# The output gate multiplied into W_out, and sums of its quarters formed early

## The chip, the cores and the metric

The kernel runs on one core of a Trainium2 chip. The metric is device time in microseconds of one execution: the median of 3 runs before the change was 1977.02 us (1976.44 to 1977.28).

The engines of the core work side by side, each through its own queue in order: TensorE (PE) multiplies matrices into PSUM, VectorE (DVE) and ScalarE (ACT) read PSUM and work on SBUF, GpSimd (POOL) works on SBUF alone, and SyncE (SP) issues the DMAs.

## The reference

```python
mod = c @ w_ada[l] + b_ada[l]
shift, scale, gate = jnp.split(mod, 3, axis=-1)
h = rms_norm(x, norm_g[l]) * (1.0 + scale[:, None, :]) + shift[:, None, :]
proj = h @ w_in[l]                       # q, k, v (512 each), u (512), z (1024)
a_out = chunk_attention(q, k, v, rel_bias[l])      # 8 heads, own chunk of 64 + 8 to the left
p_out = multiscale_pool(u, w_pool[l], pool_scale[l])
y = jnp.concatenate([a_out, p_out], axis=-1) * jax.nn.silu(z)
x = x + gate[:, None, :] * (y @ w_out[l])
```

There are 4096 tokens of 1024 channels, and everything is float32. `gate` holds one number for each output channel and is the same for all tokens.

## The kernel before

Each float32 operand of a large product is split into a rounded part (`hi`, an ACT cast) and the rest (`lo`, a subtraction on DVE or POOL); a product then takes three matmuls: hi by hi, hi by lo, lo by hi. The helper is `split` (lines 96 to 98).

**Projections (0 to about 580 us).** The tokens go in eight segments of 512. For each segment twelve projections of 24 matmuls form z and u. `load_x` loads x for the next segment, sums its squares on ACT and writes the row scales to DRAM (`rs_d`); a second DMA reads them back, spread over all partitions (`rb`). `prep` multiplies x by `rb` on POOL (L260), applies scale and shift on DVE (L261) and splits. The read-out of a projection of z is L306 on DVE. `ada` forms one eighth of scale, shift or gate from 512 KB of W_ada, on DVE (L192).

**Attention (to about 1703 us).** 64 units (half of the heads, segment, head) run with the q, k, v products of other tokens between them. In the last six units another product takes their place, the o-steps.

**The output product.** It is y (4096 x 1024) by W_out (1024 x 1024). Row blocks of 128 tokens are taken in pairs, p and p + 16, and each pair is a 2 x 2 product of blocks. The kernel forms it in Winograd's way with seven products instead of eight, from sums of quarters of y and of W_out. Two of the seven, y's upper quarters by the plain quarters of W_out, are the o-steps: 32 steps of 12 matmuls into `ps`, two for each pair. The step of the first half copies its partial sum to DRAM (`s1_d`), the second adds and stores the first output quarter. 24 of the 32 stand in attention's plan, and eight (24 to 31) behind it. The other five products (numbered 2, 1, 3, 4 and 0, 12 matmuls each, into `yps` and `zps`) run afterwards in sixteen passes of 60 matmuls. Before that, `w_prep` loads the quarters of W_out, forms their sums on DVE and POOL and splits them. Each pass fetches four blocks of y, forms sums of them on POOL (`combine`, L841 to L844), splits them, reads each product out (L864 to L874), multiplies by the gate on DVE (`finish`, L426) and adds x on POOL (L427).

Program order is not the order of execution. A scheduler with a time model places each engine's instructions ahead of the run; buffers come from pools with a fixed number of slots. The pools of the last stage lie in space that attention's tiles leave, among them the score tiles `p` (pool `b_s`).

Of the kernel before, what the change touches and what calls it, by code (L numbers as in the profile page):

```python
# [10 lines left out]
F32 = mybir.dt.float32  # L11
# [9 lines left out]
P = 128  # L21
D = 1024
# [28 lines left out]
def block_kernel(ctx, tc, x, xT, par, crow, w_adaT, w_in, w_uT, bias, w_pool, w_out, rcnt, out):  # L51
# [13 lines left out]
    gate_d = dram.tile([1, D], F32, name="gate_d")  # L65
    s1_d = [dram.tile([P, SG], F32, name=f"s1_d{i}") for i in range(NPAIR)]
# [78 lines left out]
    with ExitStack() as ca:  # L145
# [155 lines left out]
        def evac(sg, n, ps):  # L301
# [28 lines left out]
            y = wk.tile([P, SG], F32, name="yp")  # L330
            nc.vector.scalar_tensor_tensor(y, m, psc[:, g : g + 1], gzs.pop(g), op0=ALU.mult, op1=ALU.mult)
# [34 lines left out]
        nc.sync.dma_start(rc, rcnt)  # L366
        halo = [wc.tile([P, 16], F32, name=f"halo{g}") for g in range(4)]
# [3 lines left out]
        for sg in range(NSG):  # L371
            nxt = sg + 1 < NSG
            for n in range(12):
# [28 lines left out]
    gate = {}  # L402

    def load_wo(n, j, pool, stage):
        a_ = pool.tile([P, 2, 512], F32R, name="w")
        b_ = pool.tile([P, 2, 512], F32R, name="w")
        for t in range(2):
            s_ = stage()
            nc.sync.dma_start(s_, wo[:, 2 * j + t, n * 512 : n * 512 + 512])
            split(a_[:, t, :], b_[:, t, :], s_, nc.gpsimd)  # L410
            WO[n, 2 * j + t] = (a_[:, t, :], b_[:, t, :])
# [41 lines left out]
    def o_items(i):  # L453
        half, p = osteps[i]

        def one(k):
# [4 lines left out]
            wh, wl = WO[0, half * 4 + k]  # L461
# [18 lines left out]
    with ExitStack() as cb:  # L480
# [270 lines left out]
        for u in range(-1, 64):  # L751
# [21 lines left out]
            if u == 57:  # L773
                for n in range(2):
                    gate[n] = bp.tile([P, 512], F32, name=f"gate{n}")
                    nc.sync.dma_start(gate[n], gate_d[:, n * 512 : (n + 1) * 512].broadcast_to([P, 512]))
                for j in range(KT // 2):
                    load_wo(0, j, w1, stage)
                for j in range(2, 4):
                    load_wo(1, j, w1, stage)  # L780

    with ExitStack() as cd:
        w3 = cd.enter_context(tc.tile_pool(name="d_w", bufs=16))
        gp = cd.enter_context(tc.tile_pool(name="d_g", bufs=1))
        dr = cd.enter_context(tc.tile_pool(name="d_r", bufs=12))
# [3 lines left out]
        for n in range(2):  # L789
            gate[n] = gp.tile([P, 512], F32, name=f"gate{n}")  # L790
            nc.sync.dma_start(gate[n], gate_d[:, n * 512 : (n + 1) * 512].broadcast_to([P, 512]))


        WT = {t: {} for t in range(1, 5)}
        tiles = {}
        for t in (2, 1, 3, 4):
            tiles[t] = [(w3.tile([P, 2, 512], F32R, name="w"), w3.tile([P, 2, 512], F32R, name="w")) for j in range(2)]
        raws = {}

        def w_split(t, k, raw, eng):  # L800
            a_, b_ = tiles[t][k // 2]
            split(a_[:, k % 2, :], b_[:, k % 2, :], raw, eng)
            WT[t][k] = (a_[:, k % 2, :], b_[:, k % 2, :])

        def w_prep(k):
            r = {}
            for i in range(2):
                for n in range(2):
                    r[i, n] = dr.tile([P, 512], F32, name="dr")
                    nc.sync.dma_start(r[i, n], wo[:, 4 * i + k, n * 512 : n * 512 + 512])  # L810
            nc.vector.tensor_tensor(r[0, 0], r[0, 1], r[0, 0], op=ALU.subtract)
            nc.gpsimd.tensor_tensor(r[0, 1], r[1, 1], r[0, 1], op=ALU.subtract)
            nc.vector.tensor_tensor(r[1, 1], r[1, 1], r[0, 0], op=ALU.subtract)
            w_split(2, k, r[1, 1], nc.vector)
            w_split(1, k, r[0, 0], nc.vector)
            nc.gpsimd.tensor_tensor(r[1, 0], r[1, 0], r[1, 1], op=ALU.subtract)
            w_split(3, k, r[0, 1], nc.vector)
            w_split(4, k, r[1, 0], nc.gpsimd)
        WT[0] = {k: WO[1, 4 + k] for k in range(4)}

# [4 lines left out]
        RAW, SX, YP, ZP, U2, DH = {}, {}, {}, {}, {}, {}  # L825

        def fetch(p):
# [6 lines left out]
            SX[p] = s1  # L834

        def combine(t, p):

            g = nc.gpsimd
            if t == 2:
                s1 = RAW[p, 2, 0] = dr.tile([P, 4, P], F32, name="dr")  # L840
                g.tensor_tensor(s1, RAW[p, 1, 0], RAW[p, 1, 1], op=ALU.add)  # L841
                g.tensor_tensor(RAW[p, 1, 0], RAW[p, 0, 0], RAW[p, 1, 0], op=ALU.subtract)
                g.tensor_tensor(RAW[p, 0, 0], s1, RAW[p, 0, 0], op=ALU.subtract)
                g.tensor_tensor(RAW[p, 0, 1], RAW[p, 0, 1], RAW[p, 0, 0], op=ALU.subtract)  # L844
            raw = {2: RAW[p, 0, 0], 1: RAW.get((p, 2, 0)), 3: RAW[p, 1, 0], 4: RAW[p, 1, 1], 0: RAW[p, 0, 1]}[t]
            a_ = sh.tile([P, 4, P], F32R, name="bhh")
            l_ = sh.tile([P, 4, P], F32R, name="bhl")
            split(a_, l_, raw, nc.vector)
            DH[t, p] = (a_, l_)

        def step(t, p):
            b2 = p + NPAIR
# [5 lines left out]
            xr = None if t in (2, 1) else load_xr(*{3: (b2, 1), 4: (b2, 0), 0: (p, 1)}[t])  # L858
            last = nc.vector if p == NPAIR - 1 else nc.gpsimd
            a_, l_ = DH.pop((t, p))  # L860
            product(ps, a_, l_, WT[t], t in (1, 2))
            if t == 2:
                U2[p] = dc.tile([P, 512], F32, name="u2")
                nc.vector.tensor_tensor(U2[p], ps, SX[p], op=ALU.add)  # L864
            elif t == 3:
                c = op.tile([P, 512], F32, name="qkr")
                nc.vector.tensor_tensor(c, ps, SX[p], op=ALU.add)
                nc.vector.tensor_tensor(c, ZP[p], c, op=ALU.add)
                finish(c, 1, xr, b2, nc.gpsimd)
            elif t == 4:  # L870
# [68 lines left out]
```

## Time and profile before

| | |
|---|---|
| median of 3 runs | 1977.02 us |
| the profiled execution | 1978.8 us, its span 1977.0 us |
| PE busy | 1895.7 us, 96% |
| DVE, ACT, POOL busy | 64%, 46%, 48% |
| mean granted TensorE clock | 0.99 |
| HBM read, written | 158.39 MB, 62.93 MB |

The span is the time from the first to the last instruction; 1.8 us of the execution lie around it. "Busy" says how much of the span an engine had an instruction in work. PE's pieces overlap slightly, since a matmul begins before its predecessor has left the array. Where the stages differ, the share over the whole span says little, and the views of single stretches below are the ones to read.

### The profile page before, as it was taken

The numbers are of one execution on the slowest core, as the hardware profiler recorded it, in microseconds if no ns is written. First come the engines' busy times: TensorE is split into PE (matmuls) and PEld (weight loads), VectorE is DVE, ScalarE is ACT, GpSimd is POOL, SyncE is SP. The second block draws the span as 40 slices with busy tenths as digits, with TensorE's granted clock in tenths as the row PEclk, the third lists the DMA queues.
The fourth block names the chain that finished last, engine by engine and source line by source line (L and its number), as shares of the span: only waits on it lengthen the run. The fifth ranks groups of instructions, "written<-read, shape, count | busy, mean of one in ns | idle before, by whom it ended". The sixth has DMA issues, their size and how long they took to land.

```text
span 1977.0 us, 30086 instructions
## 1 busy us (share of the span) xinstructions
PE 1895.7 (96%) x10352; PEld 1625.4 (82%) x10352; DVE 1268.1 (64%) x2460; ACT 916.7 (46%) x1954; POOL 951.0 (48%) x1482
## 2 busy tenths in 40 slices
PE   6989999999999999999999999999999999779998
PEld 4767888888888898898888888888888788558887
DVE  7656554555544557666666666667666755668896
ACT  5423122212224557656666665666656765422221
POOL 6232322133036663454455556534454644587774
PEclk9999999999999999999999999999999999889999
DMA  9555254435432211121223222212121455646664
GB/s 333 194 167 170 81 151 137 160 87 164 152 115 70 65 60 54 54 65 44 65 79 93 64 68 72 65 38 65 54 60 49 125 163 164 206 159 211 218 207 139
DMA packets 178568, 231.67 MB, mean 117 GB/s; under 512 B 18160, under 2 KB 94448, under 8 KB 178416
## 3 DMA queue, kind: packets, MB, share of 16 engines
q1 hardware_dynamic: 178416, 229.77, 36.8%
q8 instruction: 81, 1.33, 0.3%
q14 instruction: 71, 0.58, 0.1%
HBM read 158.39 MB, written 62.93 MB: 112 GB/s over the span
## 4 chain that ended last, share of the span: by engine, by line
PE 81%; DVE 8%; DMA 5%; ACT 3%; issue 2%; POOL 1%; SPq 0%; DVEq 0%; POOLq 0%; ACTq 0%
PE ps L529 9%; PE ps L530 9%; PE ps L531 9%; PE ptps L657 6%; PE aps L298 3%; PE ps L298 3%; PE aps L299 3%; PE ps L299 3%; PE aps L297 3%; PE ps L297 3%; PE ops L676 3%; PE sps L617 3%; PE ops L675 3%; PE sps L618 3%; PE yps L420 2%; PE yps L421 2%
## 5 line engine op out<-in xcount | busy, mean ns | idle before, releaser
L529 PE MATMUL ps<-w,bhh 128*128 128x512 f32 (+1 forms) x1024 | 354.2, 346 | 2.7 <-ACT qkr L542 2.5
L531 PE MATMUL ps<-w,bhl 128*128 128x512 f32 (+1 forms) x1024 | 351.3, 343 | 0.0
L530 PE MATMUL ps<-w,bhh 128*128 128x512 f32 (+1 forms) x1024 | 351.3, 343 | 0.0
L664 DVE TENSOR_TENSOR ptl<-ptps,pth 128x512 fp32r<-128x512 f32 x480 | 226.0, 486 | 157.3 <-ACT pth L663 153.6
L98 POOL TENSOR_TENSOR bhl<-bhr,bhh 128x512 fp32r<-128x512 f32 x148 | 192.1, 1299 | 156.8 <-ACT bhh L97 144.4
L635 ACT ACTIVATE p<-p,mx 128x640 f32<-128x640 f32 (+4 forms) x256 | 204.6, 799 | 115.6 <-DVE mx L622 113.5
L663 ACT CAST pth<-ptps 128x512 fp32r<-128x512 f32 x480 | 193.9, 425 | 132.0 <-PE ptps L657 107.3
L622 DVE CUSTOM_DVE_ANT_0 p<-sps,nb 128x640 f32<-128x640 f32 (+4 forms) x256 | 199.0, 777 | 84.0 <-PE sps L618 80.7
L657 PE MATMUL ptps<-ident,p 128*128 128x128 f32 x1200 | 213.2, 274 | 0.3
L529 PEld LDWEIGHTS ps<-w,bhh 128*128 128x128 f32 x1024 | 193.4, 189 | 21.7 <-ACT qkr L542 3.6
L531 PEld LDWEIGHTS ps<-w,bhl 128*128 128x128 f32 x1024 | 193.5, 189 | 17.9
L530 PEld LDWEIGHTS ps<-w,bhh 128*128 128x128 f32 x1024 | 193.7, 189 | 17.5
L260 POOL TENSOR_TENSOR xt<-xt,rb 128x512 f32<-128x512 f32 x56 | 80.0, 1463 | 236.3 <-DMA rb<-rs_d 236.3
L675 PE MATMUL ops<-pth,v 128*128 128x512 f32 x480 | 162.9, 340 | 5.3 <-ACT pth L663 2.8
L617 PE MATMUL sps<-kr,qs 128*128 128x320 f32 (+2 forms) x480 | 156.2, 333 | 7.5 <-DVE mx L622 6.9
L657 PEld LDWEIGHTS ptps<-ident,p 128*128 128x128 f32 x1200 | 147.1, 140 | 19.6 <-DVE ql L582 0.7
L676 PE MATMUL ops<-ptl,v 128*128 128x512 f32 x480 | 155.6, 331 | 1.9 <-DVE ptl L664 1.2
L298 PE MATMUL aps<-hlo,w 128*128 128x512 f32 x392 | 153.8, 392 | 1.8 <-DVE hlo L98 1.8
L297 PE MATMUL ps<-hhi,w 128*128 128x512 f32 x376 | 146.9, 394 | 7.9 <-DVE gz L306 7.9
L297 PE MATMUL aps<-hhi,w 128*128 128x512 f32 x392 | 152.5, 392 | 0.2 <-ACT w L97 0.2
L299 PE MATMUL aps<-hhi,w 128*128 128x512 f32 x392 | 152.4, 392 | 0.0
L298 PE MATMUL ps<-hlo,w 128*128 128x512 f32 x376 | 147.2, 391 | 2.5 <-POOL hlo L98 2.5
(166 smaller groups left out, 4274.8 us busy)
## 6 DMA issues: line engine op xcount, KB each, us to landing
bhr<-hT_d SPq DMA_DIRECT2D x128, 256.0 KB, 2.8
xt<-in_x_dram SPq DMA_DIRECT2D x32, 512.0 KB, 4.7
qkr<-in_x_dram SPq DMA_DIRECT2D x64, 256.0 KB, 3.9
dr<-yT_d SPq DMA_DIRECT2D x64, 256.0 KB, 3.1
xt<-in_xT_dram SPq DMA_DIRECT2D x28, 512.0 KB, 6.2
hT_d<-xt SPq DMA_DIRECT2D x56, 256.0 KB, 2.3
w_s<-in_w_adaT_dram SPq DMA_DIRECT2D x16, 512.0 KB, 6.7
yT_d<-yp SPq DMA_DIRECT2D x32, 256.0 KB, 2.3
```

The source lines that it names most:

```text
L297: nc.tensor.matmul(ps, wh[:, cs], a_, start=k == 0, stop=False)
L298: nc.tensor.matmul(ps, wh[:, cs], l_, start=False, stop=False)
L299: nc.tensor.matmul(ps, wl[:, cs], a_, start=False, stop=k == KT - 1)
L529: nc.tensor.matmul(ps, a_, wh, start=k == 0, stop=False)
L530: nc.tensor.matmul(ps, a_, wl, start=False, stop=False)
L531: nc.tensor.matmul(ps, l_, wh, start=False, stop=k == KT - 1)
L617: nc.tensor.matmul(o, QS[ph, sg, h][:, qc], ks[:, k0 : k0 + n], start=True, stop=False)
L635: nc.scalar.activation(p_[:, w0:WIN], p_[:, w0:WIN], AF.Exp, scale=-1.0, bias=mx, accum_out=ls)
L657: nc.tensor.transpose(out=ps[:, i * P : (i + 1) * P], in_=Pt[ph, sg, h, i][:, w : w + P], identity=ident)
L664: nc.vector.tensor_tensor(l_[:, r], ps[:, r], a_[:, r].bitcast(F32), op=ALU.subtract)
L675: nc.tensor.matmul(o[:, r], v, a_[:, r], start=n == 0, stop=False, skip_group_check=True)
L676: nc.tensor.matmul(o[:, r], v, l_[:, r], start=False, stop=last, skip_group_check=True)
```

## The change

- `w_sums`, new: in segments 3 to 6 it loads four blocks of W_out, multiplies them by the gate (spread over the partitions in `gb`) on POOL, forms the four sums there, and stores the seven results in DRAM (`wg_d`).
- The eight `ada` calls for the gate move from segment 7 to segments 1 and 2, four each.
- `load_wo` reads ready blocks from `wg_d`; `w_prep` is gone. The last stage only loads and splits them, now on DVE.
- The gate tiles and the gate multiplies at read-out are gone. `fetch` also loads x (`xr`) and adds the partial sum `s1` to it on POOL; a read-out adds PSUM to `xr`, and the result is stored.
- The sums of y move from POOL to DVE and are formed when they are needed; fetching starts one product earlier (at product 2 instead of product 1).
- The pool tile `yp` is gone (the product with `gz` is written in place), and the pool `dr` has 14 slots instead of 12.

```diff
+        def w_sums(k):
+            r = {}
+            for i in range(2):
+                for n in range(2):
+                    r[i, n] = a_stage()
+                    nc.sync.dma_start(r[i, n], wo[:, 4 * i + k, n * 512 : n * 512 + 512])
+                    nc.gpsimd.tensor_tensor(r[i, n], r[i, n], gb[:, n * 512 : n * 512 + 512], op=ALU.mult)
+            nc.sync.dma_start(wg_d[0][k], r[0, 0])
...
+            t1, t2 = a_stage(), a_stage()
+            nc.gpsimd.tensor_tensor(t1, r[0, 1], r[0, 0], op=ALU.subtract)
+            nc.sync.dma_start(wg_d[1][k], t1)
...
+                if sg in (1, 2) and n == 1:
+                    for j in range(4):
+                        ada(xp, 12 + 4 * sg + j)
+                    if sg == 2:
+                        nc.sync.dma_start(gate_d.rearrange("o (j p) -> p (o j)", p=P), mod[:, 16:24])
+                        nc.sync.dma_start(gb, gate_d.broadcast_to([P, D]))
+                if 3 <= sg < 7 and n == 1:
+                    w_sums(sg - 3)
...
-            if not nxt:
-                for j in range(8):
-                    ada(xp, 16 + j)
...
+    def load_wo(q, pool, stage, eng):
+        W = WO[q] = {}
+        for j in range(2):
...
+                nc.sync.dma_start(s_, wg_d[q][2 * j + t])
+                split(a_[:, t, :], b_[:, t, :], s_, eng)
...
-    def finish(c, n, xr, b, eng):
-        nc.vector.tensor_tensor(c, c, gate[n], op=ALU.mult)
-        eng.tensor_tensor(c, c, xr, op=ALU.add)
...
-                    nc.vector.tensor_tensor(t, ps, gate[0], op=ALU.mult)
-                    nc.gpsimd.tensor_tensor(t, t, xr, op=ALU.add)
-                    nc.sync.dma_start(out[p * P : (p + 1) * P, 0:512], t)
+                    nc.vector.tensor_tensor(xr, ps, xr, op=ALU.add)
+                    nc.sync.dma_start(out[p * P : (p + 1) * P, 0:512], xr)
...
-        for n in range(2):
-            gate[n] = gp.tile([P, 512], F32, name=f"gate{n}")
-            nc.sync.dma_start(gate[n], gate_d[:, n * 512 : (n + 1) * 512].broadcast_to([P, 512]))
...
+            for t, b, n in ((0, p, 1), (3, p + NPAIR, 1), (4, p + NPAIR, 0)):
+                xr = XR[p, t] = load_xr(b, n)
+                nc.gpsimd.tensor_tensor(xr, xr, s1, op=ALU.add)
...
-            g = nc.gpsimd
+            g = nc.vector
             if t == 2:
                 s1 = RAW[p, 2, 0] = dr.tile([P, 4, P], F32, name="dr")
+                raw = dr.tile([P, 4, P], F32, name="dr")
                 g.tensor_tensor(s1, RAW[p, 1, 0], RAW[p, 1, 1], op=ALU.add)
...
+                g.tensor_tensor(raw, s1, RAW[p, 0, 0], op=ALU.subtract)
...
+            xr = XR[p, 0 if t == 2 else t]
+            nc.vector.tensor_tensor(xr, ps, xr, op=ALU.add)
+            if t == 3:
+                nc.vector.tensor_tensor(xr, ZP[p], xr, op=ALU.add)
...
         for i in range(24, len(osteps)):
-            if i < 28:
-                w_prep(i - 24)
+            if i in (24, 25, 27, 29):
+                load_wo({24: 2, 25: 1, 27: 3, 29: 4}[i], w3, d_stage, nc.vector)
```

The order in which the scheduler places the instructions changes with it, at three places that matter below. In the rows, `ops` is attention's output, `ps` an o-step, `yps` and `zps` the five combined products; `x2` means that the row stands twice in succession.

PE, the end of attention. Before:

```order
L675 MATMUL ops<-pth,v 128x128
L676 MATMUL ops<-ptl,v 128x128
L462 MATMUL ps<-w,bhh 128x512
L463 MATMUL ps<-w,bhh 128x512
L464 MATMUL ps<-w,bhl 128x512
```

The same place in the changed kernel:

```order
L699 MATMUL ops<-pth,v 128x128
L700 MATMUL ops<-ptl,v 128x128
L451 MATMUL yps<-w,bhh 128x512
L452 MATMUL yps<-w,bhh 128x512
L451 MATMUL zps<-w,bhh 128x512
```

The last `ops` was followed by 72 matmuls of o-steps and then by `yps`; now `yps` follows at once, and all o-steps stand inside attention.

DVE behind its last instruction of attention (L699, now L723). Before (L811 and L813 form W sums, L473 reads an o-step out, L98 splits):

```order
L699 TENSOR_TENSOR osum<-ops,osum 64x512
L811 TENSOR_TENSOR dr<-dr 128x512
L473 TENSOR_TENSOR qkr<-ps,gate_19532 128x512
L811 TENSOR_TENSOR dr<-dr 128x512
L813 TENSOR_TENSOR dr<-dr 128x512
L98 TENSOR_TENSOR w<-dr,w 128x512
L473 TENSOR_TENSOR qkr<-ps,gate_19532 128x512
L98 TENSOR_TENSOR w<-dr,w 128x512 x2
```

In the changed kernel (L100 splits, L832 to L844 form sums of y, L862 reads product 2 out):

```order
L723 TENSOR_TENSOR osum<-ops,osum 64x512
L100 TENSOR_TENSOR w<-dr,w 128x512 x8
L832 TENSOR_TENSOR dr<-dr 128x512
L833 TENSOR_TENSOR dr<-dr 128x512
L839 TENSOR_TENSOR dr<-dr 128x512
L844 TENSOR_TENSOR dr<-dr 128x512
L100 TENSOR_TENSOR bhl<-dr,bhh 128x512 x2
L100 TENSOR_TENSOR w<-dr,w 128x512
L100 TENSOR_TENSOR bhl<-dr,bhh 128x512
L100 TENSOR_TENSOR w<-dr,w 128x512 x7
L862 TENSOR_TENSOR qkr<-yps,qkr 128x512
```

No read-out of an o-step is left there; all 16 W splits, the sums and three splits of y stand ahead of the first read-out.

SP in segment 1, from the first load of x to the return of the row scales. Before:

```order
L162 DMA xt<-in_x_dram 128x1024 x4
L256 DMA xt<-in_xT_dram 128x2x512
L308 DMA gz_d_77<-gz 128x512
L256 DMA xt<-in_xT_dram 128x2x512 x3
L178 DMA rs_d_95<-rxy 128x4x1
L180 DMA rb<-rs_d_95 128x512
```

In the changed kernel:

```order
L192 DMA xt<-in_w_adaT_dram 128x1024 x4
L164 DMA xt<-in_x_dram 128x1024
L310 DMA gz_d_77<-gz 128x512
L164 DMA xt<-in_x_dram 128x1024 x3
L258 DMA xt<-in_xT_dram 128x2x512 x4
L180 DMA rs_d_95<-rxy 128x4x1
L182 DMA rb<-rs_d_95 128x512
```

Four loads of W_ada stand ahead of x, in the same four tiles `xt`.

## Rows read from the trace of the kernel before

**Rows 1.** The page: busy time by engine; PE's share in 40 slices

```profile
PE 1895.7 (96%) x10352; PEld 1625.4 (82%) x10352; DVE 1268.1 (64%) x2460; ACT 916.7 (46%) x1954; POOL 951.0 (48%) x1482
PE   6989999999999999999999999999999999779998
```

**Rows 2.** Windows: stretch, its length, engines' busy us, clock, DMA share, GB/s

```profile
350.00:400.00 50.00, 50.00 (x222) 41.40 (x221) 24.41 (x46) 13.51 (x23) 4.71 (x7) 1.00 0.44 144
600.00:1555.00 955.00, 940.45 (x5949) 835.11 (x5948) 620.33 (x1481) 585.67 (x1343) 501.83 (x1083) 1.00 0.21 63
1690.00:1703.00 13.00, 11.59 (x74) 9.42 (x73) 9.01 (x22) 8.03 (x21) 1.69 (x2) 1.00 0.13 40
1750.00:1755.00 5.00, 4.55 (x11) 3.58 (x12) 4.47 (x3) 1.44 (x3) 4.37 (x4) 0.50 0.24 82
```

**Rows 3.** PE's waits from 1690 us on: total us, times, longest

```profile
PE ps L462 <- DVE qkr L473: 12.1, 3, 6.9
PE yps L420 <- ACT bhh L97: 11.6, 1, 11.6
```

**Rows 4.** Timeline (start, length, idle before and releaser) around the end of attention

```profile
1703.08 0.28 PE L676 MATMUL ops<-ptl,v 128*128 128x128 f32 x1
1709.55 0.69 DVE L473 TENSOR_TENSOR qkr<-ps,gate 128x512 f32<-128x512 f32 x1 [2.91 <-DMA gate<-gate_d]
1750.45 0.80 PE L420 MATMUL yps<-w,bhh 128*128 128x512 f32 x1 [11.63 <-ACT bhh L97]
```

**Rows 5.** The chain that ended last: start, length, what

```profile
1752.10 0.43 PE zps L421
```

**Rows 6.** Timeline of POOL, SP and DVE, then two windows, 1702 to 1714 us

```profile
1704.83 1.26 POOL L701 TENSOR_TENSOR osum<-osum,gzb 128x512 f32<-128x512 f32 x1 [7.78 <-issue]
...
1702.22 1.29 SPq L810 DMA_DIRECT2D dr<-in_w_out_dram  x3
...
1705.48 1.16 DVE L811 TENSOR_TENSOR dr<-dr 128x512 f32<-128x512 f32 x1 [0.78 <-DMA dr<-in_w_out_dram]
...
1704.00:1706.00 2.00, 0.00 (x0) 0.00 (x0) 1.22 (x2) 0.00 (x0) 1.17 (x1) 0.54 0.82 284
...
1712.00:1714.00 2.00, 2.00 (x6) 1.52 (x6) 1.43 (x2) 0.00 (x0) 0.83 (x1) 0.50 1.07 398
```

**Rows 7.** Window of one pass in the last stage

```profile
1900.00:1913.60 13.60, 13.60 (x61) 11.26 (x60) 12.30 (x14) 3.12 (x6) 10.43 (x8) 1.00 0.65 215
```

**Rows 8.** Groups by line, 1760 to 1950 us: busy us, mean ns

```profile
L98 DVE TENSOR_TENSOR bhl<-dr,bhh 128x512 fp32r<-128x512 f32 x70 | 81.1, 1158 | 1.3 <-ACT bhh L97 1.3
L426 DVE TENSOR_TENSOR u<-u,gate 128x512 f32<-128x512 f32 x14 | 23.8, 1699 | 0.0
L864 DVE TENSOR_TENSOR u<-yps,s 128x512 f32<-128x512 f32 x14 | 9.5, 679 | 0.0
```

**Rows 9.** Timeline of SP, DVE, POOL and PE in segments 7, 1 and 2

```profile
508.45 5.77 SPq L190 DMA_DIRECT2D xt<-in_w_adaT_dram  x5
...
518.66 0.08 DVE L192 DVE_READ_ACCUMULATOR2_ANT acc<- 128x1 f32 x1
...
144.62 11.40 POOL L260 TENSOR_TENSOR xt<-xt,rb 128x512 f32<-128x512 f32 x8 [31.73 <-DMA rb<-rs_d]
...
156.68 0.67 DVE L306 TENSOR_TENSOR gz<-gz,ps 128x512 f32<-128x512 f32 x1
...
157.40 0.50 PE L297 MATMUL ps<-hhi,w 128*128 128x512 f32 x1 [1.72 <-DVE gz L306]
...
211.70 2.93 DVE L261 TENSOR_SCALAR xt<-xt,gcol,mod 128x512 f32<-128x512 f32 x2 [13.74 <-POOL xt L260]
...
223.17 0.50 PE L297 MATMUL ps<-hhi,w 128*128 128x512 f32 x1 [0.19 <-DVE gz L306]
```

**Rows 10.** DVE's timeline behind the last matmul

```profile
1971.91 0.69 DVE L874 TENSOR_TENSOR u<-zps,u 128x512 f32<-128x512 f32 x1 [1.30 <-PE zps L422]
...
1973.36 0.69 DVE L427 TENSOR_TENSOR u<-u,qkr 128x512 f32<-128x512 f32 x1
```

More of the change, by code (lines that the diff above doesn't have):

```diff
@@ L65, in block_kernel @@
     gate_d = dram.tile([1, D], F32, name="gate_d")
+    wg_d = {q: [dram.tile([P, 512], F32, name=f"wg_d{q}_{k}") for k in range(4)] for q in (0, 10, 11, 1, 2, 3, 4)}
     s1_d = [dram.tile([P, SG], F32, name=f"s1_d{i}") for i in range(NPAIR)]
@@ L329, in evac @@
                 nc.vector.tensor_tensor(m[:, 0:16], f, u[:, 16:32], op=ALU.subtract)
-            y = wk.tile([P, SG], F32, name="yp")
-            nc.vector.scalar_tensor_tensor(y, m, psc[:, g : g + 1], gzs.pop(g), op0=ALU.mult, op1=ALU.mult)
+            y = gzs.pop(g)
+            nc.vector.scalar_tensor_tensor(y, m, psc[:, g : g + 1], y, op0=ALU.mult, op1=ALU.mult)
             store_y(sg, 4 + g, y)
@@ L393, in block_kernel @@
                     load_wqkv(0, 1, lambda: a_stage(), nc.vector)
-            if not nxt:
-                for j in range(8):
-                    ada(xp, 16 + j)
-                nc.sync.dma_start(gate_d.rearrange("o (j p) -> p (o j)", p=P), mod[:, 16:24])
     op = ctx.enter_context(tc.tile_pool(name="b_qk", bufs=8))
     WO = {}
[L402 to L411, printed above, removed]
+    def load_wo(q, pool, stage, eng):
+        W = WO[q] = {}
+        for j in range(2):
+            a_ = pool.tile([P, 2, 512], F32R, name="w")
+            b_ = pool.tile([P, 2, 512], F32R, name="w")
+            for t in range(2):
+                s_ = stage()
+                nc.sync.dma_start(s_, wg_d[q][2 * j + t])
+                split(a_[:, t, :], b_[:, t, :], s_, eng)
+                W[2 * j + t] = (a_[:, t, :], b_[:, t, :])
     XP = {}
@@ L467, in one @@
                 o_load(i + 2)
-                t = op.tile([P, 512], F32, name="qkr")
                 if half == 0:
+                    t = op.tile([P, 512], F32, name="qkr")
                     nc.scalar.copy(t, ps)
@@ L773, in block_kernel @@
             if u == 57:
-                for n in range(2):
-                    gate[n] = bp.tile([P, 512], F32, name=f"gate{n}")
-                    nc.sync.dma_start(gate[n], gate_d[:, n * 512 : (n + 1) * 512].broadcast_to([P, 512]))
[L777 to L780, printed above, removed]
+                for q in (0, 10, 11):
+                    load_wo(q, w1, stage, nc.gpsimd)
     with ExitStack() as cd:
         w3 = cd.enter_context(tc.tile_pool(name="d_w", bufs=16))
-        gp = cd.enter_context(tc.tile_pool(name="d_g", bufs=1))
-        dr = cd.enter_context(tc.tile_pool(name="d_r", bufs=12))
+        dr = cd.enter_context(tc.tile_pool(name="d_r", bufs=14))
         dc = cd.enter_context(tc.tile_pool(name="d_c", bufs=3))
@@ L788, in block_kernel @@
         dz = cd.enter_context(tc.tile_pool(name="d_z", bufs=2, space=PSUM))
-        for n in range(2):
-            gate[n] = gp.tile([P, 512], F32, name=f"gate{n}")
[L791 to L819, printed above, removed]
+        d_stage = lambda: dr.tile([P, 512], F32, name="dr")
         steps = [(2, 0)]
@@ L886, in block_kernel @@
         for i, (t, p) in enumerate(steps):
-            if t == 1 and p + 1 < NPAIR:
+            if t == 2 and p + 1 < NPAIR:
                 fetch(p + 1)
```

57 lines of the change are left out of this document (30 added, 27 removed).

## The prediction, made before the change was run

> **What bounds the kernel now.** I read the page first, then the windows by stage, then PE's waits. TensorE is busy 96% of the span, so the time is PE's work plus its holes [rows 1]. In the projections PE has no hole where I looked (50.00 of 50 us from 350 on); in attention (600 to 1555 us) it is busy 940.45 of 955 [rows 2]. The holes lie in slices 1 to 3, while data first arrive, and just before the last five slices [rows 1]. Asked for 1690 us to the end, PE's waits name them: 12.1 us on DVE L473 in three pieces, the longest of 6.9, and 11.6 us in one on an ACT cast [rows 3]. Both large ones stand between the last attention matmul (1703.08 + 0.28 = 1703.36) and the first matmul of the combined products (1750.45) [rows 4]: 47.1 us.
>
> In those 47.1 us PE has 72 matmuls of the o-steps left (the order below puts 72 `ps` matmuls behind the last `ops`). At 13.60 / 60 = 0.227 us, the pitch of a pass at full clock [rows 7], they need 16.3 us. So 30.8 us are lost there: 12.1 behind L473 (first for a gate load, then behind DVE's W splits), 11.6 for the cast, which follows sums of y on POOL, and the rest in short waits and slow matmuls. The granted clock was 0.50 (1.2 GHz of 2.4) in the 5 us behind the 11.63 us hole [rows 2]; matmuls came 0.43 us apart there [rows 5].
>
> **The change part by part.**
>
> *The o-steps.* Before, L473 needs `gate`, loaded anew into space that attention frees: it runs at 1709.55, behind the gate DMA [rows 4]. Afterwards the read-out adds only `xr` and needs nothing of the last stage. The order shows what follows: all `ps` matmuls now stand before the last attention matmul. So attention ends 16.3 us later, less the holes that they fill. PE was busy 11.59 of 13.00 us from 1690 to 1703 [rows 2], 1.4 us of hole; I take 0.8 and put the end of attention at 1703.4 + 16.3 - 0.8 = 1718.9, say 1719.0 (bounds 1718 to 1722, the upper one if the o-steps' loads come late).
>
> *The first combined product.* Nothing is left for PE while W and y arrive. SP issues the W loads only behind the last store of `osum`. That chain before: POOL L701 ends at 1704.83 + 1.26 = 1706.09, 2.7 us after the last matmul [rows 6]; with SP's issue the first W load starts 3.2 us after it. The first two W loads, issued from 1702.22 on, had landed when DVE L811 started at 1705.48, so the second, about 0.43 us later, took 2.8 us [rows 6]. First landing: 6.0 us after attention. In order come 8 W loads and 4 y loads of 0.262 MB; at 398 GB/s, the rate from 1712 to 1714 [rows 6], one lands every 0.66 us, the eleventh (all that L833 needs) at 6.0 + 10 x 0.66 = 12.6. L833 (0.68 as other DVE adds without POOL) and the cast (0.62) make 13.9; with waits between three engines I take 15.0. At 284 GB/s, the rate from 1704 to 1706, it would be 18; below 13.5 it can't go, since the queue order forbids it. Products start at 1719.0 + 15.0 = 1734.0 instead of 1750.45: **-16.4 us**. The slow matmuls stand behind this hole as behind the old one.
>
> The Trainium skill ("SBUF — State Buffer", "Summary: rules for kernel authors") says to estimate HBM transfers at about 358 GB/s. The trace shows 398 here [rows 6]; by the page the eleventh load would be 0.7 us later and the sum as much smaller.
>
> *The first passes.* Behind the first splits of y DVE's row has 7 more W splits, then the read-out L862 of (2,0), for which product (3,0) waits. The last W load is the twenty-first: 6.0 + 20 x 0.66 = 19.2, plus cast and split 20.5. DVE's own work from 12.6 on is 4 sums, 3 y splits and 8 W splits, 15 x 0.68 = 10.2, so 22.8, or 25 if three POOL adds (`xr + s1`) collide with it. PE is through (2,0) and (1,0) at 15.0 + 24 x 0.227 + 12 x 0.2 (slow clock) = 22.9. So PE waits 0.6 to 3 us there, then up to 2 us more for the next y, whose loads wait for split W tiles. I take **+4 us** (0 to 8).
>
> *Steady passes.* One pass is 60 matmuls, 13.6 us of PE. Before, DVE did 13 operations in a pass and POOL 7, DVE busy 12.30 of 13.60 and PE without a hole [rows 7]. Per pass the three gate multiplies go, four y sums come to DVE: 14 operations, POOL 3. A read-out from PSUM took 0.68 to 0.69 whatever POOL did; a split, with two SBUF inputs, 1.158 on average and the `u` gate multiply 1.699 [rows 8]. Five splits and this multiply took 7.5 us a pass, 3.4 more than 6 x 0.68, beside 7 POOL operations: 0.5 per POOL operation. Now 9 x 0.68 + 5 x 0.69 + 3 x 0.5 = 11.1 us. PE covers it: 0. Below 0 it can't go, as PE has no hole there; the other bound is rival 1.
>
> *Gate into W, sums during the projections.* 28 POOL operations on idle POOL (4.71 of 50 busy at 350 to 400), 28 stores and 16 loads at DMA shares of 0.44 [rows 2]: hidden by PE, which had no hole there. They stand in POOL's queue before the next segment's `xt*rb` and, on SP, between `rs_d` and `rb`. How late may that chain be? In segment 2 L261 began at 211.70, and PE took up the eighth projection at 223.17 [rows 9]. With the fourth read-out now ahead of L261, the next to fill PSUM is the tenth projection, 2 x 24 x 0.227 = 10.9 later, at 234: 20 us and more of room, against five POOL operations of 1.3 to 1.7 and a load. I cost it 0; the bound above is rival 3.
>
> *ada moved to segments 1 and 2.* What leaves segment 7 (508 to 526 us) was hidden, in a slice of PE at 9 tenths or more [rows 1], and gives nothing. In segment 1 it costs: four W_ada loads now stand on SP before the x loads that feed `rb`. In segment 7 the last of the first four was through DVE 10.2 us after its issue (508.45 to 518.66) [rows 9]; the x loads wait for these tiles, so the chain moves by 5 to 10 us, I take 8. Before, rb's chain released POOL at 144.62; the read-out of the fourth projection came at 156.68 behind seven L261, and PE waited 1.72 us for it [rows 9]. In the new order only two L261 and one split stand before it: POOL's first multiply (1.4), two L261 (2.9, [rows 9] for two in segment 2), a split (1.7) and a cast lead to about 151.2; with the 8 it is 159.2, 2.5 us later than before: **+2.5** (-1.7 to +6).
>
> *Tail.* Before, three DVE operations follow the last matmul (1971.91 to 1974.05) [rows 10]; now one. **-1.4**.
>
> **Sum**: -16.4 + 4.0 + 2.5 - 1.4 = -11.3. The profiled run took 1978.8 us, 1.8 more than its span and than the median of 1977.02; 1978.8 - 11.3 = 1967.5, and 1.8 less on the median's scale: **1966**.
>
> **Rivals.**
> 1. *DVE bounds the passes, and it gets slower.* From a mean of 13.6 / 14 = 0.97 us per operation DVE is later than PE. If the nine two-input operations took the 1.699 of L426 [rows 8], a pass would be 9 x 1.7 + 5 x 0.69 = 18.7, 5.1 too long, 77 us in 15 passes: about 2043. With the splits' 1.158 it is 13.9, +0.3 a pass, and 1971. For it: DVE was at 90% [rows 7]. Against: the excess goes with POOL's work, which falls from 7 operations to 3. The Trainium skill ("SBUF — State Buffer", "Who interferes with whom") says that such a DVE operation and a POOL operation that reads SBUF exclude each other, the later one blocked until the other ends. By that, three POOL adds of 1.26 [rows 6] block DVE at most 3.8 us a pass: 9 x 0.68 + 5 x 0.69 + 3.8 = 13.4 of 13.6, still no bound. The trace agrees that such pairs suffer: 1.158 and 1.699 against 0.68 [rows 8].
> 2. *The hole stays.* W and y come so late that PE loses as much as before: attention's end at 1722, the first product 18 us behind it (1740, -10.4), 8 us in the first passes, 6 in segment 1, -1.4 at the tail: +2.2, so 1979, no change. For it: nothing covers the loads any more, and each of these is a bound from a row. Against: all would have to come together.
> 3. *The projections lose.* In segments 2 to 6 POOL's sums delay `rb`'s consumers until PSUM is full. For it: in segment 2 PE already waited 0.19 us for the fourth read-out [rows 9]. Against: the new order has that read-out ahead of L261. Five segments at 4 us: 1966 + 20 = 1986.
>
> **How the numbers follow.** The forecast has 0.81, rival 2 0.08, rival 1 in its slow form 0.05, rival 3 0.06. Own range of the forecast: the first product at 13.5 to 18, first passes 0 to 8, segment 1 -1.7 to +6: 1957 to 1974. With part of rival 2 the range is 1957 to 1975. A measurement of this kernel can't tell less than 0.2% (4 us) from no change: faster means below 1973. The forecast's 0.81 counts as faster (the last microsecond of its range lies above the bound and is left to rival 2); rival 2's 0.08 is the same; rivals 1 and 3 make the slower 0.11.
>
> **What would show it.** After the change the trace should have no `ps` matmul behind the last `ops`; one PE hole of about 15 us, ended by the ACT cast of `bhh`; then a short wait of `yps` on DVE L862; PE without holes in the passes; a wait of 3 to 6 us in segment 1. DVE busy in the passes near 11 of 13.6. I am wrong if PE shows a hole in each pass, or if the hole before the products is over 22 us.

## The result, and the profile after

The changed kernel takes **1987.36 us** (median of 4 runs, 1985.80 to 1990.35) against 1977.15 (1976.44 to 1977.54) for the kernel before, timed beside it: a ratio of 1.0052, 95% interval 1.0040 to 1.0064. It is slower by half a per cent; the forecast was 1966, faster, and the range (1957 to 1975) does not hold the result. The profiled run took 1988.35 us with a span of 1986.6, 9.6 more than the span before.

The page of the changed kernel, busy time and PE's slices, answers to [rows 1]. DVE and POOL have less to do, PE 4.6 us more, and slices 35 and 36 of the 40 are still the holes:

```profile
PE 1900.3 (96%) x10352; PEld 1626.1 (82%) x10352; DVE 1238.3 (62%) x2471; ACT 916.3 (46%) x1954; POOL 860.0 (43%) x1423
PE   6989999999999999999999999999999999679999
```

PE's waits of the changed kernel from 1700 us on (what waited, for what, total us, times, longest), in place of [rows 3]:

```profile
PE yps L451 <- ACT bhh L99: 17.2, 1, 17.2
PE yps L451 <- DVE qkr L862: 8.5, 2, 7.6
PE zps L453 <- DVE bhl L100: 5.8, 5, 2.0
PE yps L453 <- DVE bhl L100: 1.0, 3, 0.6
```

Of the 8.5 us behind L862, 0.9 stand in the last pass (1977.24); the kernel before has the same wait there.

PE's timeline (start, length, idle before) shows where the large ones lie; compare [rows 4]:

```profile
245.95 0.50 PE L299 MATMUL ps<-hhi,w 128*128 128x512 f32 x1 [0.34 <-ACT u L316]
254.57 0.50 PE L299 MATMUL aps<-hhi,w 128*128 128x512 f32 x1 [2.17 <-ACT hhi L99]
...
1723.15 0.27 PE L700 MATMUL ops<-ptl,v 128*128 128x128 f32 x1
1740.60 0.79 PE L451 MATMUL yps<-w,bhh 128*128 128x512 f32 x1 [17.17 <-ACT bhh L99]
...
1757.24 0.76 PE L451 MATMUL yps<-w,bhh 128*128 128x512 f32 x1 [7.60 <-DVE qkr L862]
...
1854.29 0.50 PE L453 MATMUL zps<-w,bhl 128*128 128x512 f32 x1 [1.73 <-DVE bhl L100]
```

The windows show a stretch of one segment's start, the first passes, and 100 us of steady passes (columns as in [rows 2]). In the 100 us PE issues 398 matmuls; without holes it would be 443 (it is, in the last experiments), so 45 x 0.227 = 10.2 us are lost, more than the listed waits say. DVE is far from full, 63.77 of 100, where [rows 7] had 12.30 of 13.60:

```profile
250.00:275.00 25.00, 22.75 (x92) 18.09 (x91) 12.43 (x28) 10.80 (x20) 7.00 (x8) 0.93 0.79 277
1740.60:1757.20 16.60, 8.86 (x24) 6.26 (x24) 16.57 (x14) 5.64 (x10) 13.16 (x8) 0.71 0.81 290
1840.00:1940.00 100.00, 93.26 (x398) 73.38 (x397) 63.77 (x93) 20.54 (x33) 27.23 (x21) 1.00 0.60 192
```

The balance of the two profiled spans, term by term:

| term | forecast | measured |
|---|---|---|
| projections (start of attention's first matmul, 625.46 to 630.95) | +2.5 | +5.5 |
| o-steps ahead of attention's end (1703.36 to 1723.42, less the 5.5) | +15.6 | +14.6 |
| hole before the first combined product | 15.0 long | 17.2 long |
| so the first product (1750.45 to 1740.60) | -13.9 | -9.85 |
| first passes (from the first of the 960 combined matmuls to the 61st, 16.1 to 26.5) | +4 | +10.5 |
| steady passes (from the 61st to the last, 205.0 to 215.4; 13.6 us each before; 14.1, 16.2, 16.2, 14.7, 16.2, 13.7 and 14.4 in seven of them) | 0 | +10.4 |
| tail (last matmul's start to the end, 5.5 to 4.0) | -1.4 | -1.5 |
| sum | -11.3 | +9.6 |

So the gain ahead of the products came in part, and the passes gave back more than all of it. Two views show how. First passes: DVE's groups from 1741 to 1756.4 us in the changed kernel, and POOL's from 1741 to 1757 (columns as in [rows 8], with the shapes):

```profile
L100 DVE TENSOR_TENSOR w<-dr,w 128x512 fp32r<-128x512 f32 x8 | 11.4, 1487 | 0.0
L100 DVE TENSOR_TENSOR bhl<-dr,bhh 128x512 fp32r<-128x512 f32 x3 | 4.2, 1408 | 0.0
...
L824 POOL TENSOR_TENSOR qkr<-qkr,s 128x512 f32<-128x512 f32 x8 | 13.2, 1677 | 15.9 <-ACT bhh L99 14.6 <-DMA s<-s_d 1.4
```

DVE has no idle time; its splits take 1.4 to 1.5 us beside eight POOL adds. Steady passes: the waits of SP's queue and of DVE from 1800 to 1945 us, and DVE's timeline ahead of the wait at 1854.29:

```profile
SPq L457 <- DMA out_dram<-qkr: 71.0, 21, 5.4
SPq L820 <- POOL qkr L824: 25.2, 8, 3.6
...
DVE dr L839 <- DMA dr<-yT_d: 19.2, 9, 2.9
DVE dr L832 <- DMA dr<-yT_d: 8.7, 4, 3.0
```

```profile
1852.34 0.69 DVE L839 TENSOR_TENSOR dr<-dr 128x512 f32<-128x512 f32 x1 [2.72 <-DMA dr<-yT_d]
1852.95 0.68 DVE L862 TENSOR_TENSOR qkr<-yps,qkr 128x512 f32<-128x512 f32 x1
1853.55 0.68 DVE L100 TENSOR_TENSOR bhl<-dr,bhh 128x512 fp32r<-128x512 f32 x1
```

The split that PE wants (1853.55) stands in DVE's order behind L839, a sum for a later pass, which waited 2.72 us for a y load, and behind a read-out. Before, POOL did these sums, and PE had no hole [rows 7]; whether that made the difference is tested in e7.

### The profile page after: what moved, and what is told of

The parts are those of the page before. It is cut to its first block, busy times and chain, and to the rows that moved or that the text cites. A ratio compares the mean times of both kernels' runs of the same rounds, so it can differ in the third digit from the quotient of the medians.

```text
span 1986.6 us, 30117 instructions
## 1 busy us (share of the span) xinstructions
PE 1900.3 (96%) x10352; PEld 1626.1 (82%) x10352; DVE 1238.3 (62%) x2471; ACT 916.3 (46%) x1954; POOL 860.0 (43%) x1423
## 4 chain that ended last, share of the span: by engine, by line
PE 78%; DVE 8%; DMA 7%; ACT 3%; issue 2%; POOL 1%; SPq 1%; DVEq 0%; ACTq 0%; POOLq 0%
PE ps L553 9%; PE ps L554 9%; PE ps L555 9%; PE ptps L681 6%; PE aps L300 4%; PE aps L301 4%; PE aps L299 3%; PE ps L300 3%; PE ps L301 3%; PE ps L299 3%; PE ops L700 3%; PE sps L641 3%; PE ops L699 3%; PE sps L642 3%; DMA dr<-yT_d 2%
## 5 line engine op out<-in xcount | busy, mean ns | idle before, releaser
L100 POOL TENSOR_TENSOR bhl<-bhr,bhh 128x512 fp32r<-128x512 f32 x148 | 191.1, 1292 | 177.5 <-ACT bhh L99 155.8
L699 PE MATMUL ops<-pth,v 128*128 128x512 f32 x480 | 162.9, 340 | 4.6 <-ACT pth L687 3.0
L681 PEld LDWEIGHTS ptps<-ident,p 128*128 128x128 f32 x1200 | 147.4, 140 | 19.6 <-DVE ql L606 0.7
L642 PE MATMUL sps<-kr,ql 128*128 128x320 f32 (+2 forms) x480 | 148.8, 319 | 0.0
```

What stands on the lines that cost most here:

```text
L642: nc.tensor.matmul(o, QL[ph, sg, h][:, qc], ks[:, k0 : k0 + n], start=False, stop=True)
L681: nc.tensor.transpose(out=ps[:, i * P : (i + 1) * P], in_=Pt[ph, sg, h, i][:, w : w + P], identity=ident)
L699: nc.tensor.matmul(o[:, r], v, a_[:, r], start=n == 0, stop=False, skip_group_check=True)
```

## The experiments

Eleven kernels, each made from the changed one and timed in five rounds beside the kernel before. Gains are told by the excess over the kernel before, timed beside each of them: +10.2 us for the changed kernel. The scheduler placed each kernel anew, so an edit can also move instructions that it does not name. The 100 us window of the steady passes varies by itself: in e4, whose edit lies elsewhere, PE issues 407 matmuls there where the changed kernel has 398.

| kernel | us | excess | ratio to before, 95% interval |
|---|---|---|---|
| e1, 12 slots for x | 1999.78 | +21.7 | 1.0116 (1.0101 to 1.0131) |
| e2, adds on DVE | 2007.24 | +29.2 | 1.0151 (1.0138 to 1.0164) |
| e3, o-steps behind | 1978.16 | +0.1 | 1.0002 (0.9991 to 1.0012) |
| e4, gate on POOL's queue | 1988.26 | +10.2 | 1.0063 (1.0046 to 1.0080) |
| e5, late x loads | 1982.95 | +5.0 | 1.0026 (1.0017 to 1.0035) |
| e6, W sums one segment later | 1985.51 | +7.5 | 1.0040 (1.0028 to 1.0052) |
| e7, y sums on POOL | 1997.58 | +19.6 | 1.0102 (1.0088 to 1.0117) |
| e8, e3 + e5 + e6 | 1971.58 | -6.4 | 0.9968 (0.9956 to 0.9980) |
| e9, e5 + 22 slots for y | 1974.78 | -3.0 | 0.9986 (0.9977 to 0.9994) |
| e10, 22 slots for y | 1984.72 | +6.9 | 1.0032 (1.0021 to 1.0043) |
| e11, e8 + 22 slots for y | 1962.87 | -14.9 | 0.9926 (0.9914 to 0.9939) |

**e1.** `load_xr` takes its tiles from a new pool in the last stage:

```
+        dx = cd.enter_context(tc.tile_pool(name="d_x", bufs=12))
-                xr = XR[p, t] = load_xr(b, n)
+                xr = XR[p, t] = load_xr(b, n, dx)
```

> The x tiles of the passes come from a pool of their own with 12 slots, instead of sharing 8 with the o-steps. Theory A (in the steady passes SP, which issues in order, holds each x load until an out store has landed and freed a slot, and the y loads and stores stand behind it, so DVE's sums of y start late): the waits of PE for the y splits (6.8 us in eight pieces between 1850 and 1930 us) go, DVE's idle time before L832 and L839 too; about 1980.5 us instead of 1987.4. Rival B (the passes lose because DVE and POOL collide on SBUF): nothing changes in the passes, 1987 us, or a few us more, since x loads and POOL adds run still earlier.

Both wrong: 11.5 us slower than the changed kernel, 7.5 of them from the 61st combined matmul on (222.9 us instead of 215.4). SP still waits for landed out stores, and DVE more for y. Waits of SP and DVE in e1, 1800 to 1945 us:

```profile
SPq L457 <- DMA out_dram<-qkr: 73.4, 28, 5.0
...
DVE dr L840 <- DMA dr<-yT_d: 27.0, 9, 3.9
```

The reading that fits is that the loads fill twelve slots as they filled eight, and that each then stands in SP's order close behind the store that frees its slot. Why this is slower, and not the same, was not taken apart.

**e2.**

```
-                nc.gpsimd.tensor_tensor(xr, xr, s1, op=ALU.add)
+                nc.vector.tensor_tensor(xr, xr, s1, op=ALU.add)
```

> The adds of xr + s1 go from POOL to DVE, so POOL does nothing in the last stage. Theory C (in the first passes eight POOL adds, 13.2 us of POOL, stretch ten DVE splits from 6.8 to 15.4 us, which keeps the read-out of the first product 7.6 us late and drops the clock again): the splits take 0.69 us each, PE's wait for the first read-out falls from 7.6 to under 1.5 us, and the matmuls behind it run at full clock: about 10 us less there, the passes as before (DVE 17 operations of 0.69, 11.7 of 13.6 us): 1977 us (1974 to 1983). Rival D (DVE's queue there is too long as such, or the loads of W are late): the wait stays at 5 us or more, and three more adds in DVE's queue make it 1987 to 1991.

The forecast of 1977 failed by 30 us. In the first passes theory C held all the same: seven W splits take 4.30 us together, where the changed kernel needs 9.67, and the first wait for L862 is 3.15 us, not 7.6. What is left of it is five of the adds, 3.10 us, which now stand in DVE's row ahead of the read-out (timeline of DVE and PE in e2):

```profile
1745.44 4.30 DVE L100 TENSOR_TENSOR w<-dr,w 128x512 fp32r<-128x512 f32 x7
1749.66 3.10 DVE L824 TENSOR_TENSOR qkr<-qkr,s 128x512 f32<-128x512 f32 x5
...
1753.62 0.47 PE L451 MATMUL yps<-w,bhh 128*128 128x512 f32 x1 [3.15 <-DVE qkr L862]
```

In the steady passes the adds wait for late x loads in DVE's order, and PE with them, which costs more than is gained (PE's waits from 600 to 1990 us, then DVE's from 1800 to 1945):

```profile
PE yps L451 <- DVE qkr L862: 21.9, 11, 3.9
...
DVE qkr L824 <- DMA qkr<-in_x_dram: 50.0, 18, 5.2
```

**e3.** `LASTMM[0]` is the last attention matmul; the block gives an order on PE, not a wait:

```
+                if i >= 27:
+                    with tc.issue_after(LASTMM[0]):
+                        f()
```

> The last five o-steps (60 matmuls, 13.6 us) are issued on PE behind the last attention matmul, by an order edge alone; nothing else is changed. Theory E (hoisting the o-steps took away the cover of the W and y loads): attention ends at about 1709.8 instead of 1723.4, the loads start there, the o-steps run meanwhile, and the first combined product starts at about 1727 instead of 1740.6, behind a hole of under 5 us; 13 us less, up to 16 if the matmuls behind it run at full clock: 1973 us. Rival F (the loads of W and y wait for something else than the end of attention, such as the o-steps' own read-outs or slots): the hole stays over 12 us and the time at 1984 to 1988.

Theory E holds: attention's end goes from 1723.42 to 1708.50, the first product from 1740.60 to 1728.14, behind a wait of 3.05 instead of 17.17. The time falls by 10 us, not 13: PE waits 4.69 us for y of the second pass (timeline of PE and DVE in e3).

```profile
1708.23 0.27 PE L701 MATMUL ops<-ptl,v 128*128 128x128 f32 x1
...
1728.14 0.80 PE L452 MATMUL yps<-w,bhh 128*128 128x512 f32 x1 [3.05 <-ACT bhh L99]
...
1747.55 0.79 PE L452 MATMUL yps<-w,bhh 128*128 128x512 f32 x1 [4.69 <-ACT bhh L99]
...
1743.33 0.69 DVE L863 TENSOR_TENSOR qkr<-yps,qkr 128x512 f32<-128x512 f32 x1 [4.03 <-PE yps L454]
1743.93 1.64 DVE L833 TENSOR_TENSOR dr<-dr 128x512 f32<-128x512 f32 x1
```

The trace shows why. The four y loads of that pass were issued from 1730.34 to 1733.73 and took 5.2 to 5.5 us, so y was there by about 1739. But L833, the first sum of it, stands in DVE's order behind the read-out L863 of product (3,0), and DVE stood idle for 4.03 us until PE was through that product. So it is not the load that is late here but DVE's order.

**e4.**

```
-    nc.sync.dma_start(gate_d.rearrange("o (j p) -> p (o j)", p=P), mod[:, 16:24])
-    nc.sync.dma_start(gb, gate_d.broadcast_to([P, D]))
+    nc.gpsimd.dma_start(gate_d.rearrange("o (j p) -> p (o j)", p=P), mod[:, 16:24])
+    nc.gpsimd.dma_start(gb, gate_d.broadcast_to([P, D]))
```

> The store of the gate vector and its load back (segment 2) are issued by POOL instead of SP. Theory G (SP waits 10.4 us for the gate store to land before it may issue the load back, and the store of the row sums of x for segment 3 stands behind it, ready at 202.1 us but issued at 206.9): the row sums leave some 4.7 us earlier, PE's waits at 245.95 and 254.57 us (0.34 and 2.17) and the slow matmuls behind them go, projections end 4.5 us earlier: 1983 us. Rival H (POOL's products of W, which stand ahead of POOL's products of x in segment 3, and collide with DVE, delay the chain): the waits stay within 1 us of what they are, 1987 us.

Theory G falls: no gain. PE's waits from 200 to 600 us add up to 2.4 us, where the changed kernel has 2.5, which is what rival H gives; that POOL's products are the reason, as H has it, no run shows. The row sums of segment 3 leave at 207.82 instead of 206.87, now behind the first W loads of the sums, two of which hold SP for 6.23 us (SP's timeline in e4):

```profile
200.51 6.23 SPq L377 DMA_DIRECT2D bhh<-in_w_out_dram  x2
206.84 0.94 SPq L258 DMA_DIRECT2D xt<-in_xT_dram  x1
207.82 0.60 SPq L180 DMA_DIRECT2D rs_d<-rxy  x1
```

**e5.** s1 and x loads move out of `fetch` into `fetch_x`, called just ahead of the pass's first product; `YL[1]` is the last y load of pass 1, `OUTS` the list of out stores:

```
+            if t == 2:
+                with tc.issue_after(YL[1] if p == 0 else OUTS[-min(2, p)]):
+                    fetch_x(p)
```

> The loads of s1 and of the x tiles of pass p, and with them POOL's adds, are issued on SP just before the first product of their pass: for pass 0 behind the y loads of pass 1, from then on behind the out store of the product before last; only these edges are new (8 slots as before). Theory A2 (more slots moved nothing, since the loads run ahead until every slot is taken, whatever their number; then each x load stands right behind the out store that frees its slot, and SP waits for that store to land, 71 of 145 us, with y loads behind it): the x loads now find free slots, SP's waits for landed out stores fall from 71 to under 10 us of 145, DVE's waits for y in L832 and L839 go, PE's waits for y splits (6.8 us) fall under 1 us. With theory C (POOL adds stretch the W splits of the first passes), only three adds are left near them, behind most splits: PE's wait for the first read-out goes from 7.6 to about 2 us, the clock stays up: 9 us more. Together about 1972 us (1968 to 1978). Rival B2 (y loads are late because of their own 14 slots, held by DVE's order): DVE's waits in L839 stay, and the time is 1978 (theory C alone) or more.

Theory C held once more: from 1741 to 1753.2 us DVE's W splits take 0.689 each, and PE's wait of 7.6 us for the first read-out is gone; waits of 1.45 and 1.42 us, for a cast and a split of y, come in its place (e5's groups of DVE, PE's timeline):

```profile
L100 DVE TENSOR_TENSOR w<-dr,w 128x512 fp32r<-128x512 f32 x8 | 5.0, 689 | 0.0
...
1749.41 0.50 PE L451 MATMUL yps<-w,bhh 128*128 128x512 f32 x1 [1.45 <-ACT bhh L99]
1751.56 0.80 PE L453 MATMUL yps<-w,bhl 128*128 128x512 f32 x1 [1.42 <-DVE bhl L100]
```

SP's wait for landed out stores is gone, as theory A2 had it, but the steady passes gain next to nothing (214.7 us from the 61st matmul on instead of 215.4): DVE still waits for y, and SP for DVE to free y slots (waits, 1800 to 1945 us). Rival B2 is right for the passes.

```profile
SPq L820 <- DVE dr L837: 31.8, 9, 3.8
...
DVE dr L843 <- DMA dr<-yT_d: 35.3, 10, 4.5
```

**e6.**

```
-                    if sg == 2:
+                if sg == 3 and n == 1:
-                if 3 <= sg < 7 and n == 1:
-                    w_sums(sg - 3)
+                if 4 <= sg and n == 1:
+                    w_sums(sg - 4)
```

> Gate store, gate load and the four groups of products and sums of W move one segment later each (segment 3 instead of 2 for the gate, segments 4 to 7 instead of 3 to 6 for the sums). Theory H2 (whatever queue has the gate store, the first group's two W loads, products and stores stand ahead of the row-sum chain of segment 3 on SP and POOL, and that segment has no slack: before, its projection already waited 0.19 us): at segment 4 the chain has room, so the 4.6 us lost between 246 and 260 us go: 1983 us. Rival H3 (any segment in which the sums come in loses as much): 1987 us, with the waits at some 320 us instead of 250.

Theory H2 holds in kind: the profile lists no wait of PE between 200 and 600 us any more, and attention ends at 1719.37, 4.05 earlier. 2.7 of it is left in the time; the hole and the first wait for L862 are 0.8 and 1.1 us longer.

**e7.**

```
-            g = nc.vector
+            g = nc.gpsimd
```

> The four sums of y in a pass go back to POOL, everything else as in the changed kernel. Theory A2 (the sums stand in DVE's order ahead of splits that are due, and wait there for late y loads): the y loads stay late, SP's waits stay near 70 of 145 us, but the splits that are due are no longer behind them; PE's waits for y splits in the steady passes fall from 6.8 to under 2 us. In the first passes POOL has more to do beside the W splits, so the wait for the first read-out stays at 7 to 10 us: 1982 us in all (1980 to 1986). Rival J (the passes need the sums' results that late anyway, on whichever engine): the steady waits stay at 5 us or more, 1987 to 1992 us.

Both sizes wrong: with the sums on POOL the kernel is 9.4 us slower. The hole grows to 23.6 us, a wait of 6.2 for a y split follows it (PE's waits in e7 from 600 us on), and the steady passes are no better: 219.6 us from the 61st matmul on, 402 matmuls from 1840 to 1940. So the steady loss does not go with the sums' place in DVE's queue. It is no clean test, since SP now waits for POOL's sums to free y slots (last row, 1800 to 1945 us):

```profile
PE yps L451 <- ACT bhh L99: 30.9, 7, 23.6
...
PE yps L453 <- DVE bhl L100: 9.6, 8, 6.2
...
SPq L818 <- POOL dr L833: 31.9, 9, 4.0
```

**e8.**

> The edits of the o-steps behind attention, of the late x loads and of the later W sums together. If their theories (E, A2 with C, H2) hold and add up: attention ends at about 1705.5, the first product starts at about 1723.5 behind the o-steps, and the passes from there take the 226 us that they take in the kernel before: 1950 us by the span, 1953 us in all (1948 to 1960). If y of the second pass comes late as it did with the o-steps behind attention alone (a wait of 4.7 us and slow matmuls behind it): 1960. If the x edges do not help the passes: 1970.

It beats both kernels, though only by the worst of the three cases named: the edits nearly add up (10.1, 5.2 and 2.7 us alone, 16.6 together), but the steady passes are nearly as long as in the changed kernel (214.3 us).

**e9, e10, e11.** One number more, in e5, in the changed kernel and in e8:

```
-        dr = cd.enter_context(tc.tile_pool(name="d_r", bufs=14))
+        dr = cd.enter_context(tc.tile_pool(name="d_r", bufs=22))
```

> The late x loads (1983 us by themselves) with 22 slots instead of 14 for the y tiles and sums. Theory K (a pass now takes six of these slots, four loads and two sums, so a y load is issued only when DVE frees a slot, some 5 us before DVE needs the tile, and lands too late behind x loads; DVE then waits in L843, 35 of 145 us, with splits that are due behind it): with eight more slots each y load is issued over a pass earlier, DVE's waits for y fall under 5 of 145 us, PE's waits for y splits from 8.8 to under 1.5 us: 1976 us. Rival L (as with the x slots, loads run ahead into any number of slots and stay as late): 1983 us.

> The changed kernel with 22 instead of 14 slots for the y tiles and sums and nothing else. If the y slots alone set the steady waits, these (6.8 us) go: 1981 us. If SP's waits for landed out stores (71 of 145 us, with y loads behind them) hold the y loads back as much, part of the waits stays: y loads are a pass ahead, so a delay of 4 us on SP should no longer reach DVE, and I expect 1981 to 1984 us. If neither, 1987 us. The first passes stay as they are (the wait of 7.6 us for the first read-out).

> All edits together: o-steps behind attention, late x loads, later W sums, 22 slots for y. By theory K the steady waits of the three edits together (some 8 us) go: 1964 us (1962 to 1968). By rival L nothing changes against the three edits: 1971.6 us.

Theory K holds. The window from 1840 to 1940 us in e9, then in e10:

```profile
1840.00:1940.00 100.00, 100.00 (x443) 82.81 (x442) 66.08 (x94) 22.69 (x37) 31.46 (x24) 1.00 0.57 190
```

```profile
1840.00:1940.00 100.00, 96.63 (x421) 78.18 (x420) 62.40 (x96) 21.80 (x35) 30.56 (x22) 1.00 0.59 193
```

With both edits PE has no hole left in this window, every pass takes 13.6 us, and DVE does as much as before; from the 61st matmul to the last it is 206.4 us (206.1 in e11), where the kernel before has 205.0. Either edit alone does little. With the y slots alone PE issues 421 matmuls in the window, about halfway, but the whole stretch still takes 214.1 us, in an execution 5 us above e10's median; by the medians 3.3 us are gained, and SP still waits 68.0 us for landed out stores. With the late x loads alone it is 408, no more than in e4. e11 is 25 us (1.3%) faster than the changed kernel and 0.7% faster than the one before.

## Why the prediction was wrong

The term that failed most is *steady passes*, put at 0: 10.4 us were lost there, to y that lands late. Behind it come the first passes (6.5 us more than the 4 forecast) and the W sums, put at 0 (5.1 us). (The three bounds that it names for its own range add up to 1956 to 1976.5, not 1957 to 1974; the result lies outside either.)

*What bounds the kernel, and the o-steps*: right, but for a slice (the large holes stand ahead of the last four, not five). All `ps` matmuls run ahead of attention's end, which they put off by 14.6 us (15.6 forecast).

*The first combined product*: the hole is 17.2 us, inside the bounds given (13.5 to 18). 1.9 of the 2.2 us above the 15.0 are one wait: the first W load leaves 5.1 us behind attention (1728.51), not 3.2, since SP holds it until the last store of y has landed (2.29 us), which the text left out. That nothing covers the hole was in the text; that the change itself had taken the cover away, and that five o-steps put back behind attention are worth 10 us, was not (e3).

*The first passes*, +4 forecast, +10.5 measured: the step failed in its price for a collision, "25 if three POOL adds (`xr + s1`) collide with it". Eight adds ran, and they stretched DVE's eleven splits, by their means, from 11 x 0.69 = 7.6 to 8 x 1.49 + 3 x 1.41 = 16.1 us: 8.5, or 1.1 us per add. The text took 2.2 us for its three, and 0.5 each in the steady passes, from an average over a pass in which DVE and POOL overlap only in part [rows 8]. The Trainium skill's rule that stood under rival 1 ("SBUF — State Buffer", "Who interferes with whom") says that such a pair excludes each other; by it, as an estimate, eight adds of 1.26 us [rows 6] block DVE for up to 10.1 us. The trace's 8.5 is nearer to that than to the average's 4. Without POOL beside them the W splits took 0.689 (e2, e5): shown. The collision is not all of it: without it the first passes still take 22.8 us (e2, with the adds in DVE's row) and 21.4 (e5), so it accounts for 4 to 5 of the 6.5 us above the forecast. The collision also brought a second slow stretch that the text did not have: behind the wait of 7.60 us the granted clock was 0.50 again (1757.3 to 1760.4), and product (3,0) took 4.43 us instead of 2.72.

*Steady passes*, 0 forecast, +10.4 measured: this step failed most. "11.1 us. PE covers it: 0" is no worse than cautious as a sum (DVE was busy 63.77 of 100 us) and says nothing of when. The sign that the text gave for being wrong, holes in the passes, came in seven of them. The runs show y landing just in time or late: DVE waits for it at L839 and L832 (27.9 of 145 us), and, in order, hands the delay on to splits that were ready (1852 to 1854 us). The x loads stand in the same queue as the y loads, each behind the store that frees its slot; SP waits 71.0 of 145 us for such stores, against 13.5 in the kernel before. And a pass takes six y slots where it took five, though of 14 instead of 12. e9 shows that the two together are what costs: with later x loads and more y slots the window has no hole, with the same DVE work and the sums still in DVE's row. Either alone gave little (e5, e10), and how the loss divides between them stays open. That the sums went from POOL's queue to DVE's is not shown to be the reason: moved back, they bring nothing (e7, which has a cost of its own). Rival 1 (DVE as the bound) was the wrong theory for the right place: its price comes from work, and this is a matter of when loads land.

*Gate into W, sums during the projections*, 0 forecast, 5.1 us measured, all at the start of segment 3: the projection that starts at 239.63 in the kernel before starts 0.4 us later, at 240.01, and the one at 261.39 starts 5.5 us later, at 266.88. The step looked for room at the right chain, but took the wrong limit for it. Timeline of SP before, then of SP and POOL after:

```profile
197.38 0.37 SPq L178 DMA_DIRECT2D rs_d<-rxy  x1
205.68 0.34 SPq L180 DMA_DIRECT2D rb<-rs_d  x1
...
206.87 0.54 SPq L180 DMA_DIRECT2D rs_d<-rxy  x1
217.66 0.33 SPq L182 DMA_DIRECT2D rb<-rs_d  x1
...
216.54 1.29 POOL L383 TENSOR_TENSOR bhh<-bhl,bhh 128x512 f32<-128x512 f32 x1
222.66 11.67 POOL L262 TENSOR_TENSOR xt<-xt,rb 128x512 f32<-128x512 f32 x8 [4.83 <-DMA wg_d<-bhh]
```

On SP the first W loads, behind a gate store that took 10.4 us, stand ahead of the row sums, so `rb` leaves 12 us later. That is within the 20 us until PSUM would fill, but PE wants the split x of segment 3 sooner than that, and waits for it at 254.57. This is rival 3's place, in one segment of five, but not its mechanism: POOL was through with its first five W operations and stood idle for 4.83 us before its first `xt*rb` (the row names a store of W sums that landed at 222.65; `rb` itself landed 4.8 us behind its issue, at 222.4). The 1986 that the rival gave lies near the result by accident. Moved one segment on, the same work loses nothing there (e6): shown. Which of the queued pieces costs what was not taken apart.

*ada*, +2.5 forecast: about 0. In segment 1 the wait of 1.72 us [rows 9] is gone, and a new one of 0.98, for a split on DVE, stands at 126.50. After the first 60 us PE was 1.2 us later than before, 0.67 of them from a first x tile that came later (16.17 to 16.84); at 240 us it was 0.4.

*Tail*, -1.4: -1.5 measured, one DVE operation (1983.00) behind the last matmul where [rows 10] had three.

What stays open: why the first passes still take 5 to 7 us more than before when the collision is gone (e2, e5) and when the o-steps cover the hole as well (22.5 us in e11). In e11 PE's waits of 1.97 us for a cast of y and 1.42 for a split lie in that stretch. Before the first of them DVE goes straight from six W splits into the sums of the second pass (1735.39), without waiting for y, so there too its order, and not the landing of y, comes last; no run varied that order.

## What to carry to other kernels

When an operation moves to another engine's queue, count not only its microseconds but what it waits for and who stands behind it in the new order; an average of busy time can't show either. Then test the suspicion: here the sums in DVE's row looked guilty, but moved back they cost 9 us more, and y that came in time cured the steady passes. A load that reuses a slot is as late as the last user of that slot, and holds up what its queue has behind it. More slots did not help where the release is a store's landing (x, e1); for y they gave 3 us alone and 8 us once the x loads were out of the way (e9 against e5). And before work is moved out of a stretch, ask what it was covering there.

## What was not expected of the hardware

A DVE operation with two SBUF inputs took 0.69 us alone (e5) and 1.49 on average beside back-to-back POOL adds, and these 1.68 instead of 1.26 [rows 6]: both lose, DVE more. A store of 1024 single elements (the gate vector) took 10.4 us to land, one of 256 KB (y) 2.29. The chain of waits of the changed kernel has both:

```profile
193.51 10.40 DMA gate_d<-mod
...
1726.14 2.29 DMA yT_d<-osum
```
